# Merge stores of 64 rows, q and k laid channel by channel, and the merge weights on ScalarE's queue, in a dilated-attention decoder step

## The chip, the cores and the metric

The kernel is one program on one core of a Trainium2 chip. The metric is the device time of one execution in microseconds. The core has a matrix engine (TensorE, PE in the profile, with its weight loads as PEld), three engines for elementwise work (VectorE as DVE, ScalarE as ACT, GpSimd as POOL) and SyncE (SP), which here does nothing but issue transfers. Transfers run on sixteen DMA engines. SP and ACT can issue them; an issue stands in the issuing engine's instruction order, and an instruction that must wait holds up all that are behind it on its engine.

## What is computed

One layer of a decoder over a prompt of 2048 rows of 1024 and a sample group of 32 rows, all in fp32. The part that matters here is the attention of the prompt: eight heads of 64 channels, each with three dilated windows whose outputs are merged by their softmax denominators.

```python
q, k, v, u, vg = _project(x, norm1_g, w_in)
q, k, v = _heads(q), _heads(k), _heads(v)
for (w, d), bias_hj in zip(BRANCHES, biases):      # (128, 1), (512, 4), (2048, 16)
    o, l = _dilated_prompt(q, k, v, bias_hj, d, w // d + 1)
    outs.append(o)
    lses.append(l)
att = _merge_branches(outs, lses).reshape(B, S, D_ATT).astype(x.dtype)
...
x = x + jnp.concatenate([att, u * gate], axis=-1) @ w_out
x = x + _swiglu(x, norm2_g, w_gate, w_up, w_down)
```

## The kernel before

**Precision.** Operands of a matmul are split into a high part and a low remainder, and products of the parts are added up. q and k of a head are kept as parts of 64 channels each; a tile of 128 partitions holds two such parts, so that one matmul over 128 partitions gives two of the products. `qh` holds q's high part twice, `k` holds k's high and low part, `ql` holds q's low part twice. The sum over partitions does not depend on their order as long as all three tiles use the same one.

**Stages.** The input projection comes first (to about 661 us). It leaves q and k transposed in DRAM (`qk_d`, by part, 512 channels, 2048 positions), the values in `v_d`, and the gated half of the concatenation in `cat_d`. Then comes attention, head by head; then the output projection; then the feed-forward layer, which takes most of the rest.

**Attention.** A head is 20 items: 16 blocks of 128 queries of the first two windows together (the band; at most 640 keys each) and 4 strided items of the third window. Each item passes through scores (TensorE), bias and minimum (VectorE, lines 818 and 885 to 888, the last on GpSimd), exponential (ScalarE, lines 823 and 891), transposes (TensorE) whose results ScalarE and VectorE split into parts (`ph`, `pl`; lines 844 and 849), and products with the values (TensorE, lines 863 and 911). Four band blocks together give 512 columns of output. ScalarE copies them into `ob` (line 872): one tile of 128 x 2048 for each head, with two buffers, so head h writes the buffer that head h - 2 used. The upper and the lower 64 partitions of `ob` are products with the two parts of the values and are added much later, when the output projection reads them.

**The merge.** When a head's sums are complete, during the next head, two weights for each position are worked out (`weights_a`, `weights_b`), written to DRAM (`f_d`, line 959) and read back spread over all partitions, in four chunks of 512 positions (`merge_load`, line 967). GpSimd multiplies and adds for each chunk (lines 974 to 978), and `merge_store` (line 981) writes the chunk to `cat_d`.

**Order.** A planner holds (step, phase, function) and emits everything in that order, so the order on every engine is fixed when the program is built. One step is one item. Within a step the phases come as: early, exp, low, scores, turn, mid, values, out, misc, store. The loads of head h + 1 are emitted at steps 2 to 13 of head h, the merge of head h in steps 8 to 24 after its last item; that is, its last store stands at step 4 of head h + 2. All of these are transfers of SP's queue, one behind the other: loads of q, k, the bias table `b` and the values, the store of the weights, the merge loads and the merge stores.

**Output projection.** Eight units of 128 rows for each half of the columns of `w_out`. `load_cat` (line 1224) reads a block of `cat_d` in three transfers, `split_cat` adds the two halves and splits them. The first half of `w_out` is loaded during head 7 into `pair` buffers, the second half during the units, through the two `fr` buffers (line 1202). The last head is merged during these units, by VectorE and GpSimd in turn, chunk by chunk.

Of the kernel before, what the change touches and what calls it, by code (L numbers as in the profile page):

```python
# [10 lines left out]
F32 = mybir.dt.float32  # L11
# [8 lines left out]
P = 128  # L20
T = 2048
NT = T // P
D = 1024
KD = D // P
H = 8
C = 64
DA = 512
# [11 lines left out]
def dap(t, offset, pattern):  # L39
    return bass.AP(tensor=t.tensor, offset=t.offset + offset, ap=pattern)  # L40


class Plan:
# [21 lines left out]
def hymba_step(ctx: ExitStack, tc: tile.TileContext, A: dict, O: dict):  # L65
    nc = tc.nc
    sync, act, dve, pool, pe = nc.sync, nc.scalar, nc.vector, nc.gpsimd, nc.tensor
# [3 lines left out]
    dram = ctx.enter_context(tc.tile_pool(name="dram", bufs=1, space=DRAM))  # L71
# [27 lines left out]
    qk_d = dram.tile([2, 2, DA, T], F32, name="qk_d")  # L99
    v_d = dram.tile([T, H, 2, C], F32, name="v_d")  # L100

    cat_d = dram.tile([D + DA, T], F32, name="cat_d")
    f_d = dram.tile([H, 2, T], F32, name="f_d")
    l12_d = dram.tile([H, 768], F32, name="l12_d")
    l3_d = dram.tile([H, 256], F32, name="l3_d")
    b12_d = dram.tile([H, P, 640], F32, name="b12_d")
    b3_d = dram.tile([H, P, P], F32, name="b3_d")
    cs_d = dram.tile([SR, D], F32, name="cs_d")
    zs_d = dram.tile([3, SR, DA], F32, name="zs_d")

# [36 lines left out]
    at = plan.at  # L147
# [13 lines left out]
    def raw_tile():  # L161
        return rp.tile([P, 512], F32, name="raw", tag="raw", bufs=RAW)
# [141 lines left out]
    zn = {}  # L304
# [84 lines left out]
        act.activation(so, pt, AF.Copy)  # L389

    def store_gated(g, ct):
        sync.dma_start(cat_d[DA + ct * P:DA + (ct + 1) * P, g * 512:(g + 1) * 512], zn.pop(("so", g, ct)))

    def sample_rows(kind, ps):

# [53 lines left out]
        sync.dma_start(dst, l_)  # L449

    def table_spread():
        sync.dma_start(b12_d, dap(l12_d, 127, [[768, H], [-1, P], [1, 640]]))
        sync.dma_start(b3_d, dap(l3_d, 127, [[256, H], [-1, P], [1, P]]))
# [179 lines left out]
    for j in range(8):  # L633
        s0 = 105 + 4 * j if j < 3 else 117 + 3 * (j - 3) if j < 6 else 127 + 3 * (j - 6)
# [22 lines left out]
    for half in range(2):  # L657
        for ki, kind in enumerate(ORDER[half]):
            for gi, tiles in enumerate(GROUPS):
                start = ((half * 5 + ki) * 3 + gi) * 8  # L660
                for k in range(KD):
                    if start == 0:

                        for j in range(3):
                            n = 3 * k + j
# [6 lines left out]
                for j, tj in enumerate(tiles):  # L672
# [17 lines left out]
                    else:  # L690
# [24 lines left out]
    for i, (b, t, u) in enumerate(key_units):  # L715
        s0 = key_steps[i]
# [11 lines left out]
    for bg in range(2):  # L728
        s0 = V0 - 8 + bg * 33
# [31 lines left out]
    def value_tile(n):  # L761

        if n % 4 == 1:
            return hev.tile([P, NT, 2 * C], F32R, name="ve", tag="v", bufs=1)
        return hv.tile([P, NT, 2 * C], F32R, name="v", tag="v", bufs=3)

    def load_head(h):

        d = heads[h] = {}
        rows = slice(h * C, (h + 1) * C)  # L770
        qk = hev if h % 2 == 0 else hod
        for nm, w_, parts in (("qh", 0, (0, 0)), ("k", 1, (0, 1)), ("ql", 0, (1, 1))):
            t_ = d[nm] = qk.tile([P, T], F32R, name=nm, tag="qk", bufs=3)
            for s in range(2):
                sync.dma_start(t_[s * C:(s + 1) * C, :].bitcast(F32), qk_d[w_, parts[s], rows, :])
                yield
        b_ = row_tile("b")
        d["b3"], d["b12"] = b_[:, 640:768], b_[:, 0:640]
        sync.dma_start(d["b3"], b3_d[h])
        sync.dma_start(d["b12"], b12_d[h])  # L780
        yield
        if h == 0:

            t_ = d["vb"] = value_tile(2 * h + 1)
            for n0, n1 in ((0, 10), (10, NT)):
                sync.dma_start(t_[:, n0:n1].bitcast(F32), dap(v_d, n0 * P * H * 2 * C, [[H * 2 * C, P], [P * H * 2 * C, n1 - n0], [1, 2 * C]]))
                yield
# [168 lines left out]
        dve.tensor_mul(f[:, 0:2, :], f[:, 0:2, :], m.unsqueeze(1).broadcast_to([P, 2, NT]))  # L956

    def weights_store(h, f):
        sync.dma_start(dap(f_d, h * 2 * T, [[NT, P], [T, 2], [1, NT]]), f[:, 0:2, :])


    mf = {}

    def merge_load(h, ch):
        f1, f3 = mf[h, ch] = (raw_tile(), zn_tile())
        for z, t_ in enumerate((f1, f3)):
            sync.dma_start(t_, dap(f_d, (h * 2 + z) * T + ch * 512, [[0, P], [1, 512]]))

    def merge(h, ch, eng, part=None):
# [7 lines left out]
        if part in (None, 2):  # L977
            eng.tensor_add(x, x, y)

    def merge_store(h, ch):  # L980
        sync.dma_start(dap(cat_d, h * C * T + ch * 512, [[D * T, 2], [T, C], [1, 512]]), obs[h][:, ch * 512:(ch + 1) * 512])


    sgu = {}
# [48 lines left out]
    NI = len(OTHER)  # L1033
    L = B0 + len(items) - 1
    at(222, "misc", begin, 0)
    for y in range(7):
        at((222, 222, 224, 224, 226, 226, 228)[y], "misc", load, 0)
    at(232, "misc", load, 0)
    at(B0 + 3, "early", load, 0)
    at(B0 + 3, "store", load, 0)  # L1040
    for h in range(1, H):

        s0 = B0 + (h - 1) * NI
        at(s0 + 1, "misc", begin, h)
        for y in (2, 2, 3, 3, 4, 5, 5, 11, 13):
            at(s0 + y, "misc", load, h)
    for h in range(H):

        s0 = B0 + (h + 1) * NI
        end = h == H - 1  # L1050
        steps = ((2, "early"), (2, "turn"), (3, "early"), (4, "early"), (5, "early"), (5, "early")) if end else (
            (3, "misc"), (4, "misc"), (5, "early"), (6, "misc"), (7, "misc"), (7, "store"))
        for (y, ph), fn in zip(steps, (lambda h=h: stats_a(sts[h]), lambda h=h: stats_b(sts[h]), lambda h=h: stats_c(h, sts[h]),
                                       lambda h=h: fs.update({h: weights_a(h, sts[h])}), lambda h=h: weights_b(h, sts[h], fs[h]),
                                       lambda h=h: weights_store(h, fs[h]))):
            at(s0 + y, ph, fn)
        if not end:

            for ch, (a, b, c) in enumerate(((8, 11, 15), (8, 14, 18), (10, 17, 21), (14, 20, 24))):
                at(s0 + a, "misc", merge_load, h, ch)  # L1060
                for part in range(3):
# [137 lines left out]
    def load_wo(B, half, s2, staged):  # L1199
        raws["o", half, s2] = w_ = staged()  # L1200
        r0 = rows_of(2 * s2)
        sync.dma_start(w_.rearrange("p (a c) -> p a c", a=2),
                       A["w_out"][r0:r0 + 2 * P, half * 512:(half + 1) * 512].rearrange("(a p) c -> p a c", p=P))
# [188 lines left out]
    def last_load(ch):  # L1392

        x, m = last[ch] = (fraw(), None)
        for z, r0 in enumerate((3 * P, D + 3 * P)):
            sync.dma_start(x[:, z * 512:(z + 1) * 512], cat_d[r0:r0 + P, ch * 512:(ch + 1) * 512])

    def last_split(ch):
# [6 lines left out]
        else:  # L1405
            split_sb(B.xh[:, 7, 512:1024], B.xl[:, 7, 512:1024], x[:, 0:512], eng_lo=dve)

    at(L - 13, "early", last_head_free)
# [30 lines left out]
    at(U0 + 6, "misc", lambda: [sync.dma_start(g_, dap(A[nm], 0, [[0, P], [1, D]])) for g_, nm in zip(gain, ("norm2_g", "final_g"))])  # L1439
    for ch in range(2):  # L1440
        at(U0 + 7 + ch, "misc", last_load, ch)
# [202 lines left out]
```

## Time and profile before

| | |
|---|---|
| median of 3 runs | 2908.54 us (2903.59 to 2911.81) |
| profiled execution | 2907.21 us |
| its span | 2905.4 us |
| mean granted TensorE clock | 0.958 |
| PE / PEld busy | 92% / 78% |
| DVE / ACT / POOL busy | 41% / 26% / 29% |
| DMA queue of SP | 356.38 MB, 39.9% of sixteen engines' span |
| DMA queue of ACT | 8.92 MB, 1.2% |

The span runs from the first to the last instruction. A busy share is a mean over stages with different limits. A line number is that of the kernel before; where a helper does the work for several callers it is the helper's line. A wait is told as what waited, for what, the sum, how often, and the longest.

### The profile page before, as it was taken

What the parts mean: (1) busy time and instruction counts of PE and PEld (TensorE: products, weight loads), DVE (VectorE), ACT (ScalarE), POOL (GpSimd) and SP (SyncE); (2) the same over time, 40 slices, a digit from 0 to 9 for tenths busy, and PEclk for the clock granted to TensorE, in tenths of its full rate; (3) what the DMA queues carried; (4) which work ended last, traced back from release to release, by engine and by line L of the source; (5) the groups of instructions that cost most, each with busy time, mean ns of one, the idle gap of its engine ahead of it and who ended that gap; (6) DMA issues with size and microseconds to landing.
All of it is one profiled execution on the core that took longest, in us unless ns stands there. A gap on an engine that the chain in (4) does not pass through costs nothing.

```text
span 2905.4 us, 33754 instructions
## 1 busy us (share of the span) xinstructions
PE 2680.6 (92%) x13058; PEld 2256.7 (78%) x13058; DVE 1198.6 (41%) x2287; ACT 762.7 (26%) x1426; POOL 848.9 (29%) x558
## 2 busy tenths in 40 slices
PE   8988888988887885999999999997999999999997
PEld 6776666667886773788888888875799999999996
DVE  3267774325766663522222222244432222222224
ACT  5323243435665661301000100022310000000002
POOL 1034642121432442122332232211032222222222
PEclk9999999998998887999999999998999999999999
DMA  7754834577665645232232223226132222222211
GB/s 239 214 177 137 265 108 132 179 207 200 170 171 151 181 144 163 95 102 87 100 104 100 87 94 110 87 76 206 39 116 88 94 95 88 87 87 87 88 44 60
DMA packets 290565, 367.45 MB, mean 126 GB/s; under 512 B 19399, under 2 KB 216184, under 8 KB 285284
## 3 DMA queue, kind: packets, MB, share of 16 engines
q1 hardware_dynamic: 285284, 356.38, 39.9%
q10 hardware_dynamic: 5120, 8.92, 1.2%
q8 instruction: 103, 1.69, 0.2%
q14 instruction: 58, 0.48, 0.1%
HBM read 309.88 MB, written 125.47 MB: 150 GB/s over the span
## 4 chain that ended last, share of the span: by engine, by line
PE 68%; DVE 10%; DMA 7%; ACT 4%; issue 3%; SPq 2%; POOL 1%; ACTq 0%; DVEq 0%; POOLq 0%
PE ps_o L1336 17%; PE ps_s L1310 12%; PE ps_s L1311 11%; PE ps_s L1312 11%; DVE pl L849 2%; PE ps_o L863 2%; PE ps_s L296 1%; DMA fr<-in_w_out_dram 1%; PE ps_s L297 1%; PE ps_s L298 1%; DVE e L818 1%; PE ps_s L812 1%; PE ps_o L1250 1%; PE ps_o L1252 1%; PE ps_o L1251 1%
## 5 line engine op out<-in xcount | busy, mean ns | idle before, releaser
L1310 PE MATMUL ps_s<-xh,gh 128*128 128x352 f32 (+1 forms) x1760 | 624.1, 355 | 0.0
L1312 PE MATMUL ps_s<-xh,gl 128*128 128x352 f32 (+1 forms) x1760 | 620.3, 352 | 0.0
L1311 PE MATMUL ps_s<-xl,gh 128*128 128x352 f32 (+1 forms) x1760 | 619.5, 352 | 0.0
L1336 PE MATMUL ps_o<-dw,hw 128*128 128x512 f32 x2112 | 500.9, 397 | 8.6 <-DVE acc L1338 8.5
L1336 PEld LDWEIGHTS ps_o<-dw,hw 128*128 128x128 f32 x2112 | 396.5, 189 | 108.1 <-DVE acc L1338 14.5
L1314 ACT ACTIVATE zn<-ps_s 128x352 f32<-128x352 f32 (+1 forms) x110 | 57.1, 519 | 1319.0 <-PE ps_s L1312 1319.0
L1315 DVE TENSOR_TENSOR zn<-zn,ps_s 128x352 f32<-128x352 f32 (+1 forms) x110 | 64.6, 588 | 722.4 <-ACT zn L1314 722.4
L1310 PEld LDWEIGHTS ps_s<-xh,gh 128*128 128x128 f32 x1760 | 332.0, 189 | 33.5
L1311 PEld LDWEIGHTS ps_s<-xl,gh 128*128 128x128 f32 x1760 | 331.2, 188 | 31.6
L1312 PEld LDWEIGHTS ps_s<-xh,gl 128*128 128x128 f32 x1760 | 330.3, 188 | 32.4
L1338 DVE TENSOR_TENSOR acc<-acc,ps_o 128x512 f32<-128x512 f32 x352 | 241.0, 687 | 214.6 <-PE ps_o L1336 214.6
L126 POOL TENSOR_TENSOR hw<-zn,hw 128x512 fp32r<-128x512 f32 (+2 forms) x110 | 119.8, 1089 | 662.0 <-DVE hw L125 662.0
L126 POOL TENSOR_TENSOR gl<-fr,gh 128x1024 fp32r<-128x1024 f32 x88 | 212.8, 2442 | 131.4 <-ACT gh L123 131.4
L126 POOL TENSOR_TENSOR dw<-fr,dw 128x1024 fp32r<-128x1024 f32 x44 | 106.5, 2420 | 377.7 <-DVE dw L125 377.7
L296 PE MATMUL ps_s<-wh,xh 128*128 128x512 f32 x480 | 200.6, 418 | 7.6 <-ACT xh L123 6.4
L297 PE MATMUL ps_s<-wl,xh 128*128 128x512 f32 x480 | 194.8, 406 | 5.6 <-DVE wl L208 5.6
L298 PE MATMUL ps_s<-wh,xl 128*128 128x512 f32 x480 | 193.8, 404 | 0.0
L296 PEld LDWEIGHTS ps_s<-wh,xh 128*128 128x128 f32 x480 | 94.5, 197 | 38.1 <-issue 9.2
L297 PEld LDWEIGHTS ps_s<-wl,xh 128*128 128x128 f32 x480 | 94.8, 198 | 25.0 <-DVE wl L208 7.4
L298 PEld LDWEIGHTS ps_s<-wh,xl 128*128 128x128 f32 x480 | 94.3, 196 | 21.3 <-DVE xl L126 0.2
L849 DVE TENSOR_TENSOR pl<-ps_t,ph 128x384 fp32r<-128x384 f32 (+2 forms) x152 | 69.5, 475 | 77.8 <-ACT ph L844 77.7
L823 ACT ACTIVATE e<-e,st 128x640 f32<-128x640 f32 (+4 forms) x128 | 96.3, 752 | 2.1 <-DVE st L818 2.0
(323 smaller groups left out, 4084.3 us busy)
## 6 DMA issues: line engine op xcount, KB each, us to landing
out_ks_dram<-in_cache_k_dram SPq DMA_DIRECT2D x56, 512.0 KB
out_vs_dram<-in_cache_v_dram SPq DMA_DIRECT2D x56, 512.0 KB
fr<-in_w_gate_dram SPq DMA_DIRECT2D x44, 512.0 KB
fr<-in_w_up_dram SPq DMA_DIRECT2D x44, 512.0 KB
fr<-in_w_down_dram SPq DMA_DIRECT2D x44, 512.0 KB
raw<-in_w_in_dram SPq DMA_DIRECT2D x72, 256.0 KB
qk_d<-pair SPq DMA_DIRECT2D x64, 256.0 KB
kv<-in_cache_k_dram SPq DMA_DIRECT2D x64, 192.0 KB
```

The lines of the kernel that those rows point to most:

```text
L126: (eng_lo or pool).tensor_sub(lo, src, hi.bitcast(F32))
L296: pe.matmul(o[j], xh[:, k, :], wh, start=(k == 0), stop=False)
L297: pe.matmul(o[j], xh[:, k, :], wl, start=False, stop=False)
L298: pe.matmul(o[j], xl[:, k, :], wh, start=False, stop=(k == KD - 1))
L823: act.activation(e[:, 0:w], e[:, 0:w], AF.Exp, bias=st[:, 0, n:n + 1], scale=-1.0, accum_out=st[:, 1, n:n + 1])
L849: dve.tensor_sub(lo, p, hi.bitcast(F32))
L1310: pe.matmul(ps[:, q_, 0:n], wh[:, ks], B.xh[:, k, a:b], start=(k == 0), stop=False)
L1311: pe.matmul(ps[:, q_, 0:n], wh[:, ks], B.xl[:, k, a:b], start=False, stop=False)
L1312: pe.matmul(ps[:, q_, 0:n], wl[:, ks], B.xh[:, k, a:b], start=False, stop=(k == KD - 1))
L1315: dve.tensor_mul(sg[:, 0:n], sg[:, 0:n], ps[:, 1, 0:n])
L1336: pe.matmul(ps[0:nr], l_, r_[:, cs], start=(z == 0 and y == 0), stop=(z == FC - 1 and y == len(ops) - 1))
L1338: dve.tensor_add(B.acc[i][0:nr, cs], B.acc[i][0:nr, cs], ps[0:nr])
```

## The change

- `merge_store` writes a whole head at once (the last head still by chunks), in two transfers: 64 rows of the upper and 64 of the lower half of `ob`. Before, each chunk was one transfer whose outermost dimension was the two halves.
- `load_head` loads each of `qh`, `k` and `ql` in one transfer to 128 partitions. The two parts of a channel lie in neighbouring partitions; before, each part was a transfer to 64 partitions. The bias tables of a head lie together in DRAM (`b_d`) and are one transfer.
- `weights_store` and, for heads 0 to 6, `merge_load` are issued by ACT. A merge load brings both weights of a chunk in one transfer, into a `pair` buffer (two of them).
- Steps: loads of q, k, b at 1 to 4 and of the values at 13 and 15; the weights one to two steps earlier; merge loads at 11, 11, 16 and 19, the merge parts from 13, 16, 19 and 22 (two later), the store at 25.
- The rows of `cat_d` are reordered (gated part first), so `load_cat` reads gated and merged rows in one transfer and the low part in a second.
- The first half of `w_out` passes through a value buffer in place of `pair`, with its loads and splits at other steps.

A head then has 13 transfers in place of 23: 3 for q and k, 1 for b, 2 for values, 1 to store and 4 to load weights, 2 to store the merged output.

```diff
-    b12_d = dram.tile([H, P, 640], F32, name="b12_d")
-    b3_d = dram.tile([H, P, P], F32, name="b3_d")
+    b_d = dram.tile([H, P, 768], F32, name="b_d")
...
-            for s in range(2):
-                sync.dma_start(t_[s * C:(s + 1) * C, :].bitcast(F32), qk_d[w_, parts[s], rows, :])
-                yield
+            sync.dma_start(t_.bitcast(F32), dap(qk_d, ((w_ * 2 + parts[0]) * DA + h * C) * T,
+                                                [[T, C], [(parts[1] - parts[0]) * DA * T, 2], [1, T]]))
+            yield
...
-        sync.dma_start(d["b3"], b3_d[h])
-        sync.dma_start(d["b12"], b12_d[h])
+        sync.dma_start(b_[:, 0:768], b_d[h])
...
     def weights_store(h, f):
-        sync.dma_start(dap(f_d, h * 2 * T, [[NT, P], [T, 2], [1, NT]]), f[:, 0:2, :])
+        act.dma_start(dap(f_d, h * 2 * T, [[NT, P], [T, 2], [1, NT]]), f[:, 0:2, :])
...
     def merge_load(h, ch):
-        f1, f3 = mf[h, ch] = (raw_tile(), zn_tile())
-        for z, t_ in enumerate((f1, f3)):
+        if h < H - 1:
+            f = pair_tile(F32)
+            mf[h, ch] = (f[:, 0], f[:, 1])
+            act.dma_start(f, dap(f_d, h * 2 * T + ch * 512, [[0, P], [T, 2], [1, 512]]))
+            return
+        mf[h, ch] = (raw_tile(), zn_tile())
+        for z, t_ in enumerate(mf[h, ch]):
             sync.dma_start(t_, dap(f_d, (h * 2 + z) * T + ch * 512, [[0, P], [1, 512]]))
...
-    def merge_store(h, ch):
-        sync.dma_start(dap(cat_d, h * C * T + ch * 512, [[D * T, 2], [T, C], [1, 512]]), obs[h][:, ch * 512:(ch + 1) * 512])
+    def merge_store(h, c0, c1):
+        for z in range(2):
+            r0 = DA * (z + 1) + h * C
+            sync.dma_start(cat_d[r0:r0 + C, c0 * 512:c1 * 512], obs[h][z * C:(z + 1) * C, c0 * 512:c1 * 512])
...
-        for y in (2, 2, 3, 3, 4, 5, 5, 11, 13):
+        for y in (1, 2, 3, 4, 13, 15):
             at(s0 + y, "misc", load, h)
...
-            (3, "misc"), (4, "misc"), (5, "early"), (6, "misc"), (7, "misc"), (7, "store"))
+            (2, "misc"), (3, "misc"), (4, "early"), (4, "misc"), (5, "misc"), (6, "mid"))
...
-            for ch, (a, b, c) in enumerate(((8, 11, 15), (8, 14, 18), (10, 17, 21), (14, 20, 24))):
-                at(s0 + a, "misc", merge_load, h, ch)
+            for ch, (a, b) in enumerate(((11, 13), (11, 16), (16, 19), (19, 22))):
+                at(s0 + a, "mid", merge_load, h, ch)
                 for part in range(3):
                     at(s0 + b + part, "store", merge, h, ch, pool, part)
-                at(s0 + c, "store", merge_store, h, ch)
+            at(s0 + 25, "store", merge_store, h, 0, 4)
...
-        for dst, r0, n in ((parts[0], DA, 4), (parts[1], 0, na), (m, D, na)):
+        for dst, r0, n in ((parts[0], 0, 4), (parts[1], DA, na), (m, D, na)) if staged else ((r, 0, ns), (m, D, na)):
             sync.dma_start(dst[:, 0:n], cat_d[r0:r0 + n * P, t0:t0 + P].rearrange("(s p) t -> p s t", p=P))
...
+    def first_stage(s2):
+        if s2 == 0:
+            stage["w"] = value_tile(2 * H).rearrange("p n c -> p (n c)").bitcast(F32)
+        return stage["w"][:, s2 % 2 * D:(s2 % 2 + 1) * D]
...
-    for s2 in range(4):
-        at(L - 12 + 3 * s2, "misc", load_wo, B, 0, s2, square_tile)
-        at(L - 9 + 3 * s2, "misc", split_wo, B, 0, s2, gate_tiles)
+    for s2, (a, b) in enumerate(((-12, -9), (-12, -7), (-8, -4), (-6, -2))):
+        at(L + a, "misc", lambda s2=s2: load_wo(B, 0, s2, lambda: first_stage(s2)))
+        at(L + b, "misc", split_wo, B, 0, s2, gate_tiles)
...
-        at(U0 + s + 1, "misc", merge_store, h, ch)
+        at(U0 + s + 1, "misc", merge_store, h, ch, ch + 1)
```

More of the change, by code (lines that the diff above doesn't have):

```diff
@@ L391, in store_gated @@
     def store_gated(g, ct):
-        sync.dma_start(cat_d[DA + ct * P:DA + (ct + 1) * P, g * 512:(g + 1) * 512], zn.pop(("so", g, ct)))
+        sync.dma_start(cat_d[ct * P:(ct + 1) * P, g * 512:(g + 1) * 512], zn.pop(("so", g, ct)))
     def sample_rows(kind, ps):
@@ L451, in table_spread @@
     def table_spread():
-        sync.dma_start(b12_d, dap(l12_d, 127, [[768, H], [-1, P], [1, 640]]))
-        sync.dma_start(b3_d, dap(l3_d, 127, [[256, H], [-1, P], [1, P]]))
+        sync.dma_start(b_d[:, :, 0:640], dap(l12_d, 127, [[768, H], [-1, P], [1, 640]]))
+        sync.dma_start(b_d[:, :, 640:768], dap(l3_d, 127, [[256, H], [-1, P], [1, P]]))
     def sample_table_load():
@@ L769, in load_head @@
         d = heads[h] = {}
-        rows = slice(h * C, (h + 1) * C)
         qk = hev if h % 2 == 0 else hod
@@ L1035, in hymba_step @@
     at(222, "misc", begin, 0)
-    for y in range(7):
-        at((222, 222, 224, 224, 226, 226, 228)[y], "misc", load, 0)
+    for y in (222, 224, 226, 228):
+        at(y, "misc", load, 0)
     at(232, "misc", load, 0)
@@ L1394, in last_load @@
         x, m = last[ch] = (fraw(), None)
-        for z, r0 in enumerate((3 * P, D + 3 * P)):
+        for z, r0 in enumerate((DA + 3 * P, D + 3 * P)):
             sync.dma_start(x[:, z * 512:(z + 1) * 512], cat_d[r0:r0 + P, ch * 512:(ch + 1) * 512])
@@ L1406, in last_split @@
             split_sb(B.xh[:, 7, 512:1024], B.xl[:, 7, 512:1024], x[:, 0:512], eng_lo=dve)
+    stage = {}
+    def first_stage(s2):
+        if s2 == 0:
+            stage["w"] = value_tile(2 * H).rearrange("p n c -> p (n c)").bitcast(F32)
+        return stage["w"][:, s2 % 2 * D:(s2 % 2 + 1) * D]
     at(L - 13, "early", last_head_free)
-    for s2 in range(4):
-        at(L - 12 + 3 * s2, "misc", load_wo, B, 0, s2, square_tile)
-        at(L - 9 + 3 * s2, "misc", split_wo, B, 0, s2, gate_tiles)
+    for s2, (a, b) in enumerate(((-12, -9), (-12, -7), (-8, -4), (-6, -2))):
+        at(L + a, "misc", lambda s2=s2: load_wo(B, 0, s2, lambda: first_stage(s2)))
+        at(L + b, "misc", split_wo, B, 0, s2, gate_tiles)
     at(L + 1, "misc", lambda: load_cat(B, 0, 7, (raw_tile(), raw_tile(), zn_tile())))
```

## The prediction

> **What bounds the kernel now.** I read the busy time by stretches first, then who waited for whom in the attention stage, then the transfer queue's own timeline, then the chain of waits around the out-projection. The changed functions work only in two of these stretches: attention (661 to about 1075 us) and the out-projection behind it (to about 1200 us); the feed-forward stage from there on is untouched. By stretches (window; its length, then busy time of PE, weight load, DVE, ACT, POOL; then the granted clock, the busy share of the 16 DMA engines, and GB/s):
>
> ```profile
> span 2905.4 us, 33754 instructions
> ...
> 940.00:990.00 50.00, 42.47 (x266) 38.67 (x265) 34.13 (x87) 31.72 (x77) 19.28 (x16) 0.91 0.68 175
> 1120.00:1160.00 40.00, 11.23 (x39) 8.05 (x39) 7.06 (x7) 3.89 (x4) 9.99 (x5) 0.68 0.42 146
> 735.00:738.00 3.00, 3.00 (x24) 3.00 (x23) 1.88 (x5) 2.64 (x7) 2.26 (x2) 1.00 1.03 340
> 766.00:771.00 5.00, 5.00 (x37) 4.95 (x36) 4.28 (x13) 4.43 (x11) 0.00 (x0) 1.00 0.98 210
> 782.50:792.70 10.20, 9.36 (x37) 8.82 (x38) 5.96 (x13) 6.56 (x15) 3.36 (x3) 0.50 0.58 166
> 1012.00:1022.00 10.00, 9.45 (x64) 8.50 (x62) 7.46 (x20) 7.48 (x19) 7.35 (x6) 1.00 0.14 54
> ```
>
> TensorE sets the pace in both, and it has holes: 7.5 us in 940 to 990, 28.8 us in 1120 to 1160. The last four rows are what transfers cost. In 735 to 738 rows of 2 KB go to 128 partitions at 340 GB/s with all engines busy. In 766 to 771 only q and k parts are moving, 64 partitions a transfer, and the same full engines give 210 GB/s. In 1012 to 1022 mostly merge stores are left, and a share of 0.14 is two engines of sixteen. And behind a hole the clock is at 0.50 for 10 us. The holes in attention have one cause:
>
> ```profile
> PEld ps_o L911 <- ACT ob L872: 32.2, 6, 7.7
> PE ps_o L911 <- ACT ob L872: 30.9, 6, 7.5
> ```
>
> PE waits (31 us of idle time, seen by both its halves; us in total, times, longest) for ScalarE's copy of the first band outputs into ob. That copy has a long wait of its own. On the transfer queue, then ScalarE, for head 6:
>
> ```profile
> 955.61 7.76 SPq L981 DMA_DIRECT2D cat_d<-ob  x3
> 963.46 3.71 SPq L775 DMA_DIRECT2D qh<-qk_d  x2
> 967.26 1.18 SPq L775 DMA_DIRECT2D k<-qk_d  x2
> 968.50 0.59 SPq L775 DMA_DIRECT2D ql<-qk_d  x1
> 969.18 0.53 SPq L981 DMA_DIRECT2D cat_d<-ob  x1
> 969.82 9.31 SPq L775 DMA_DIRECT2D ql<-qk_d  x1
> ```
> ```profile
> 969.18 22.15 DMA cat_d<-ob
> ...
> 991.44 0.60 ACT L872 ACTIVATE ob<-ps_o 128x512 f32<-128x512 f32 x1 [9.17 <-DMA cat_d<-ob]
> ```
>
> ob has two buffers, so head 6 may write its ob only when head 4's last store has landed. That store of 256 KB takes 22 us: it stands behind three others on the same two engines (a store alone at 54 GB/s is 4.9 us) and behind five half-loads of q and k. ScalarE stands from 982.27 to 991.44.
>
> What a head costs without this is read from DVE, whose bias instruction over 128 columns opens each head:
>
> ```profile
> 757.17 0.28 DVE L818 CUSTOM_DVE_ANT_0 e<-ps_s,b 128x128 f32<-128x128 f32 x1
> ...
> 962.62 0.28 DVE L818 CUSTOM_DVE_ANT_0 e<-ps_s,b 128x128 f32<-128x128 f32 x1
> ...
> 1014.71 0.81 DVE L818 CUSTOM_DVE_ANT_0 e<-ps_s,b 128x640 f32<-128x640 f32 x1
> ...
> 1016.05 0.28 DVE L818 CUSTOM_DVE_ANT_0 e<-ps_s,b 128x128 f32<-128x128 f32 x1
> ...
> 1059.15 0.81 DVE L818 CUSTOM_DVE_ANT_0 e<-ps_s,b 128x640 f32<-128x640 f32 x1
> ```
>
> ```profile
> L818 DVE CUSTOM_DVE_ANT_0 e<-ps_s,b x128: 278/812/817, 662.1 to 1059.2; 128x640 f32<-128x640 f32 x96, 128x128 f32<-128x128 f32 x8, 128x256 f32<-128x256 f32 x8, 128x384 f32<-128x384 f32 x8
> ```
>
> Head 7, which loads no further head and so does not wait, takes 43.1 us from first to last of them; 1.3 us more (1014.71 to 1016.05) leads to the next head: 44.4. Heads 2 to 6 take 258.9 together, 51.8 each. The surplus is 258.9 - 5 x 44.4 = 36.9 us: the wait itself and the slow clock behind it.
>
> **The change part by part.** *Merge store.* Four stores of 128 rows of 2 KB (outer dimension 2) become two of 64 rows of 8 KB, one step later, when all four chunks are merged. The nearest row for 64 partitions and 8 KB is 766 to 771: 210 GB/s with all engines at work, so 1.05 MB takes 5.0 us and not four times 4.9. Bounds: 340 GB/s (3.1 us) if the halves overlap, 54 GB/s (19.4 us) if the engines are again two; I take 210, the row of the same shape. The Trainium skill (DMA: Bandwidth & Descriptors, "Why a DMA increments its semaphore by 16 and not by 1") gives the engine count as the largest number up to 16 that divides the slowest dimension of both sides: 2 before, 16 after. By it the store goes as here, by the two-engine row as in rival 4; the share of 0.14 agrees with its 2.
>
> *q and k.* Six transfers to 64 partitions become three to 128, channels of both parts alternating; 3.15 MB at 210 is 15.0 us, at 340 it is 9.3. No row shows 8 KB rows to 128 partitions; 340 has the same partitions, 210 the same row length. I take 340: a longer row is no reason for a slower transfer, so the halved partitions are the likelier cause of the 210. The Trainium skill (SBUF — State Buffer, "Door 1: The DMA port swizzle") has 64 partitions reach only 8 of the 16 ports, which would make the 128-partition transfer about twice as fast; 210 against 340 leans that way.
>
> ```profile
> 1140.89 0.38 SPq L1202 DMA_DIRECT2D fr<-in_w_out_dram  x1
> ```
> ```profile
> 1144.40 1.06 ACT L123 ACTIVATE woh<-fr 128x1024 fp32r<-128x1024 f32 x1 [6.89 <-DMA fr<-in_w_out_dram]
> ```
>
> *When does the store land?* Times from the head's first bias. SP can issue q and k when the head before has made its last scores, about -2 (its last bias instruction stands at -1.3, 1014.71 above); at 340 they and the 0.39 MB of bias are through by -2 + 10.5 = +9. Beside its bytes a transfer takes some 2 us: w_out in the next stage is issued at 1140.89 and awaited to 1144.40, and 0.52 MB at 340 are 1.5 of these 3.5. The last merge now needs POOL's work two steps later, behind the strided subtraction:
>
> ```profile
> 965.41 1.29 POOL L978 TENSOR_TENSOR ob<-ob,o 128x512 f32<-128x512 f32 x1
> 969.65 1.06 POOL L888 TENSOR_TENSOR e<-e,st 128x512 f32<-128x512 f32 x1 [2.95 <-DVE st L887]
> ```
>
> That subtraction ends at 970.71, +8.1; two merge parts of 1.3 follow, so the store is issued at +11, moves until +16.5, and lands at +18.5 with the 2 us of completion. ScalarE asks at 982.27, +19.7, and PE notices only 2 us after that (the wait is 9.17 long, PE's longest 7.5). So the wait goes, with 1 to 3 us to spare. At 210 for q and k they end at +15, the store at +22: ScalarE would stand 2.5 us, PE hardly 1. Gain here: 36.9 us. The lower bound is a loss: with two engines the store lands at +32.5 where it now lands at 991.33, +28.7, and 3.8 us over five heads are 19. The upper bound has heads 0 and 1 also at 44.4 (they take 757.2 - 662.1 = 95.1 together, 6 over): 43.
>
> *Weights store and merge loads on ScalarE.* Five issues a head, in an in-order engine with the exponentials and the ph copies behind them, on which PE's values wait.
>
> ```profile
> L497 ACTq DMA_DIRECT2D qb<-zs_d x32: 357/358/602, 142.1 to 375.0; - x32
> L123 ACT ACTIVATE gh<-pair x4: 1043/1058/1079, 1035.6 to 1059.5; 128x1024 fp32r<-128x1024 f32 x4
> ```
>
> At 0.36 us an issue it is 1.8 us a head, 12.6 for seven heads if nothing hides it. ScalarE is idle 18 us of the 50 above, half of it the wait itself, and head 7, my yardstick, carries four copies of 1.06 us that other heads don't have: I take 0 beyond the yardstick, and 12.6 as the end of the range. SP loses 15 issues a head; it bounds nothing but the loads it holds back, which is counted above.
>
> *Order of loads.* Values come two steps later and are used in the next head; b is one transfer; statistics move one or two steps ahead at their old distances. The first half of w_out is staged in a value buffer because pair now holds the merge weights; its splits end two steps earlier. The bias tables of DRAM move the same bytes in the same rows. All 0; without cover the largest is a value load (1.05 MB, 3.1 us, once a head).
>
> *Out-projection.* Here the last head still stores by chunk, and the same two engines hold up what is queued behind:
>
> ```profile
> 1116.23 1.04 SPq L981 DMA_DIRECT2D cat_d<-ob  x2
> 1117.31 5.51 SPq L967 DMA_DIRECT2D raw<-f_d  x1
> ...
> 1124.70 0.38 SPq L1202 DMA_DIRECT2D fr<-in_w_out_dram  x1
> ...
> 1141.37 1.04 SPq L981 DMA_DIRECT2D cat_d<-ob  x2
> 1142.46 4.43 SPq L1439 DMA_DIRECT2D norm_g<-in_norm_g_dram  x1
> ...
> 1147.56 0.51 SPq L1202 DMA_DIRECT2D fr<-in_w_out_dram  x1
> ```
> ```profile
> 1135.20 1.06 ACT L123 ACTIVATE wol<-fr 128x1024 fp32r<-128x1024 f32 x1 [22.62 <-DMA fr<-in_w_out_dram]
> ...
> 1159.18 1.06 ACT L123 ACTIVATE wol<-fr 128x1024 fp32r<-128x1024 f32 x1 [13.71 <-DMA fr<-in_w_out_dram]
> ```
>
> With two more store issues (1 us) but no 5.51, w_out is issued at about 1120. The data ahead of it since 1114 and itself, 3.3 MB (one cat load, one x block, stores, merge weights), is 10.6 us: it lands at 1126 and not 1135, -9. The next follows POOL's subtraction behind it, also 9 earlier; then four store issues and two gains take 3.5 us instead of 6.7, and 2.6 MB, 7.7 us, land by 1140 and not 1159: -19 in all. PE then finds its clock down as before. I take -18; ends -8 (only the two long issues go) and -24 (the 28.8 idle us above, less one load's 5). The unstaged cat loads lose one issue of 0.5 us each, 15 of them; I take -1.
>
> Sum against the profiled 2907.2 (span 2905.4 and 1.8 around it; 1.3 below the median of the runs shown): 2907 - 37 - 18 - 1 = **2851 us**.
>
> **The rivals.**
> 1. *The stall shrinks only.* The store moves a step later and in one piece, so if POOL or the loads are late it lands near +25, ScalarE stands 5 us and PE 3, and the clock still drops. Of 36.9 about 20 stay: 2871. For it: a margin of 1 to 3 us. Against: two bounds for the loads both end before +22.
> 2. *ScalarE inherits the waits.* Its merge load waits for the landed weights store, and the third and fourth for POOL to give back a pair buffer.
>
> ```profile
> SPq L967 <- DMA f_d<-f: 57.0, 7, 12.0
> POOL ob L974 <- DMA raw<-f_d: 81.7, 6, 16.9
> ```
>
> SP waited up to 12 us for that landing and POOL up to 16.9 us for merge weights; on SP this harmed little, on ScalarE it stops the softmax. The store is now issued near +10 and asked for near +20, so 12 us would cost 2 us; with some POOL lateness 4 us a head: 7 x 4 = 28 given back, 2879. By the Trainium skill (DMA: Bandwidth & Descriptors, "Issuing engines are not separate DMA queues") all queues share the sixteen engines, which speaks for this one; that the engines are idle by then speaks against.
> 3. *Slower.* The same place at its worst: if merge weights issued at +20 take 20 us to land, POOL frees the first pair buffer two parts later, at +42.6, and ScalarE, which asks for it at step 16, near +32, stands 10 us a head: +70 against -56, 2921. It decides from 8 us a head (56 / 7). For it: the 16.9 above. Against: 0.5 MB at 340 GB/s is 1.6 us.
> 4. *It doesn't do what it says.* If 64 rows still go by two engines, the 1.05 MB takes 19.4 us, all at the end: the 19 us of loss above and no gain in the out-projection, 2926. Against: the 64-row loads kept all engines busy.
>
> **How the numbers follow.** Forecast 0.65 (2851), rival 1 0.15, rival 2 0.14, rival 3 0.04, rival 4 0.02. The likeliest's own range: 2834 (43 and 24 gained, and 6 for a clock that stays up) to 2866 (the 12.6 unhidden, or the smaller gain in the out-projection). Reaching into rivals 1 and 2 gives 2834 to 2882. Faster than 0.3% (9 us, what can be told here from no change): 0.91; within 0.03, the far end of rival 2; slower 0.06, rivals 3 and 4.
>
> **What would show it.** Two cat_d<-ob transfers a head; no ScalarE wait on them at L872's counterpart; heads 1 to 6 at 43 to 46 us from first bias to first bias; q and k stretches near 340 GB/s; no half clock in the middle of heads; PE busy well over 11 us in the forty that now hold 28.8 idle. Wrong, if ScalarE shows multi-microsecond waits before a merge load, if stores keep a share near 0.14, or if the heads stay over 48.

## The result

The changed kernel takes 2872.4 us (median of 4 runs, 2870.4 to 2874.0) against 2906.1 us for the one before on the same chip (4 runs, 2903.6 to 2911.8): a ratio of 0.9881, 95% interval 0.9863 to 0.9899. It is faster, by 33.7 us; the forecast was 2851. The profiled execution took 2874.0 us with a span of 2872.2, which is 33.2 below the span of before.

Where the time went is read as before, by stretches (window; length; busy time of PE, weight load, DVE, ACT, POOL; granted clock; share of the 16 DMA engines; GB/s). Kernel after:

```profile
span 2872.2 us, 33608 instructions
...
940.00:990.00 50.00, 44.76 (x287) 41.39 (x286) 35.11 (x91) 34.98 (x84) 21.29 (x19) 0.93 0.60 177
953.00:960.00 7.00, 6.91 (x40) 6.12 (x40) 6.04 (x19) 3.45 (x11) 0.99 (x1) 1.00 0.96 356
964.00:971.00 7.00, 6.25 (x29) 6.26 (x30) 3.33 (x7) 5.48 (x13) 2.54 (x3) 0.55 0.50 109
1120.00:1160.00 40.00, 37.49 (x158) 29.30 (x157) 19.17 (x36) 12.04 (x21) 4.74 (x2) 0.94 0.38 122
```

The out-projection window that held 11.23 us of PE work now holds 37.49 (all of that stage has also moved forward). q, k and the bias move at 356 GB/s, not 210. But the attention window has gained only 2.3 us of PE work, and there is still a stretch at a clock of 0.55. The waits of the attention stage (650 to 1075 us) say what became of the old stall and what is new (waiting instruction, what it waited for; us in total, times, longest). Kernel after:

```profile
POOL ob L977 <- DMA pair<-f_d: 24.0, 3, 8.7
...
ACT e L889 <- POOL e L886: 21.9, 6, 4.5
...
PE ps_t L898 <- ACT e L889: 10.4, 4, 3.3
...
POOL ob L977 <- DVE f L953: 7.0, 1, 7.0
...
POOL ob L977 <- DVE dd L950: 6.3, 1, 6.3
...
ACT ob L870 <- PE ps_o L861: 5.4, 11, 1.5
```

The copy into ob (L870, L872 before) no longer waits for any store, so the old stall is gone. In its place POOL waits for merge weights, ScalarE's strided exponential (L889) for POOL, and PE's transposes (L898) for ScalarE. The waits of 7.0 and 6.3 us, in heads 4 and 5, stand at the same merge as the other three. The profile puts them down to DVE, but that merge reads only the loaded weights and `ob`, so they count with the 24.0: 37.3 us in five waits. In head 6, in order of time, first SP's and ScalarE's queue, then the engines:

```profile
947.79 0.56 SPq L773 DMA_DIRECT2D qh<-qk_d  x1
948.44 0.56 SPq L773 DMA_DIRECT2D k<-qk_d  x1
949.05 0.60 SPq L773 DMA_DIRECT2D ql<-qk_d  x1
...
966.64 1.12 SPq L986 DMA_DIRECT2D cat_d<-ob  x2
```
```profile
948.74 0.37 ACTq L966 DMA_DIRECT2D pair<-f_d  x1
```
```profile
961.77 1.26 POOL L977 TENSOR_TENSOR ob<-ob,pair 128x512 f32<-128x512 f32 x1 [7.78 <-DMA pair<-f_d]
962.99 1.04 POOL L886 TENSOR_TENSOR e<-e,st 128x512 f32<-128x512 f32 x1
```
```profile
964.06 0.63 ACT L889 ACTIVATE e<-e 128x512 f32<-128x512 f32 x1 [4.52 <-POOL e L886]
```
```profile
964.75 1.11 PE L898 MATMUL ps_t<-ident,e 128*128 128x128 f32 x4 [3.31 <-ACT e L889]
```

This is the new wait from end to end. The merge weights of the last chunk (0.5 MB) are issued at 948.74, among 3.15 MB of q and k of the next head, and POOL can use them 13.0 us later, at 961.77. POOL executes in order; behind this merge stands the subtraction L886, which the softmax of the running head needs. So ScalarE stands 4.5 us, PE 3.3, and then the clock falls (964 to 971 above). It happens once in each of heads 2 to 6.

A head is timed as in the prediction, from DVE's bias instructions; the out-projection by DVE's twenty-fourth sum (L1258 before, L1263 after). Kernel after, then before:

```profile
760.59 0.28 DVE L816 CUSTOM_DVE_ANT_0 e<-ps_s,b 128x128 f32<-128x128 f32 x1
...
999.11 0.28 DVE L816 CUSTOM_DVE_ANT_0 e<-ps_s,b 128x128 f32<-128x128 f32 x1
...
1043.97 0.81 DVE L816 CUSTOM_DVE_ANT_0 e<-ps_s,b 128x640 f32<-128x640 f32 x1
...
1185.47 0.68 DVE L1263 TENSOR_TENSOR acc<-acc,ps_o 128x512 f32<-128x512 f32 x1
```
```profile
1217.94 0.68 DVE L1258 TENSOR_TENSOR acc<-acc,ps_o 128x512 f32<-128x512 f32 x1
```

Heads 2 to 6 take 999.11 - 760.59 = 238.5 us (258.9 before), head 7 takes 44.9 (43.1), and from head 7's last bias to the sum are 1185.47 - 1043.97 = 141.5 (1217.94 - 1059.15 = 158.8). The same three stretches were read in the profile of every experiment; the names of the kernels are explained in the next section, each where it is described:

| kernel | median us | ratio to before (95%) | heads 2 to 6 | head 7 | out-projection |
|---|---|---|---|---|---|
| before | 2906.1 | | 258.9 | 43.1 | 158.8 |
| after | 2872.4 | 0.9881 (0.9863 to 0.9899) | 238.5 | 44.9 | 141.5 |
| store_only | 2854.1 | 0.9812 (0.9795 to 0.9829) | 218.1 | 43.1 | 139.4 |
| qk_only | 2879.7 | 0.9901 (0.9885 to 0.9918) | 235.2 | 43.1 | 158.7 |
| store_and_qk | 2848.0 | 0.9789 (0.9771 to 0.9807) | 218.1 | 43.1 | 142.2 |
| two_engines_heads | 2969.5 | 1.0211 (1.0190 to 1.0232) | 306.6 | 59.9 | 159.3 |
| two_engines_last | 2881.5 | 0.9913 (0.9892 to 0.9935) | 238.1 | 45.5 | 156.0 |
| merge_earlier | 2853.1 | 0.9809 (0.9794 to 0.9825) | 218.4 | 46.3 | 140.3 |
| merge_behind | 2862.7 | 0.9847 (0.9833 to 0.9862) | 228.5 | 46.6 | 141.5 |
| qk_later | 2853.9 | 0.9819 (0.9804 to 0.9833) | 222.9 | 45.5 | 140.1 |
| merge_on_sp | 2856.9 | 0.9827 (0.9813 to 0.9842) | 220.4 | 45.9 | 146.3 |
| store_and_split_order | 2848.2 | 0.9791 (0.9776 to 0.9805) | 218.2 | 43.1 | 141.2 |
| earlier_and_split_order | 2850.3 | 0.9799 (0.9783 to 0.9815) | 218.3 | 46.2 | 135.9 |
| store_order_merge | 2850.6 | 0.9794 (0.9781 to 0.9808) | 218.3 | 43.1 | 138.0 |

### The profile page after: what moved, and what is told of

Read it like the earlier page. It is cut to its first block, busy times and chain, and to the rows that moved or that the text cites. A ratio compares the mean times of both kernels' runs of the same rounds, so it can differ in the third digit from the quotient of the medians.

```text
span 2872.2 us, 33608 instructions
## 1 busy us (share of the span) xinstructions
PE 2680.6 (93%) x13058; PEld 2260.2 (79%) x13058; DVE 1197.0 (42%) x2287; ACT 762.5 (27%) x1426; POOL 849.5 (30%) x558
## 4 chain that ended last, share of the span: by engine, by line
PE 71%; DVE 8%; DMA 6%; ACT 4%; issue 4%; POOL 2%; SPq 1%; ACTq 0%; POOLq 0%; DVEq 0%
PE ps_o L1341 17%; PE ps_s L1315 12%; PE ps_s L1316 12%; PE ps_s L1317 12%; PE ps_s L295 2%; PE ps_s L296 2%; PE ps_s L297 2%; DVE pl L847 1%; PE ps_o L1255 1%; PE ps_o L1257 1%; PE ps_o L1256 1%; PE ps_s L810 1%; DMA fr<-in_w_out_dram 1%; PE ps_o L861 1%; PE ps_t L838 1%
## 5 line engine op out<-in xcount | busy, mean ns | idle before, releaser
L816 DVE CUSTOM_DVE_ANT_0 e<-ps_s,b 128x640 f32<-128x640 f32 (+4 forms) x128 | 93.4, 730 | 3.8 <-PE ps_s L810 3.8
```

The source lines that it names most:

```text
L816: dve.tensor_tensor_reduce(e[:, 0:w], s[:, c0:c0 + w], d["b12"][:, 640 - w:640], 1.0, BIG, OP.add, OP.min, st[:, 0, n:n + 1])
```

## The experiments

**The store alone** (store_only). The kernel before with one edit:

```
 def merge_store(h, ch):
-    sync.dma_start(dap(cat_d, h * C * T + ch * 512, [[D * T, 2], [T, C], [1, 512]]), obs[h][:, ch * 512:(ch + 1) * 512])
+    for z in range(2):
+        r0 = D * z + h * C
+        sync.dma_start(cat_d[r0:r0 + C, ch * 512:(ch + 1) * 512], obs[h][z * C:(z + 1) * C, ch * 512:(ch + 1) * 512])
```

> The kernel before, with one edit: each chunk's merge store goes as two transfers of 64 rows (2 KB a row), and nothing else of the change. Theory S (the store on two engines is the cause of both old losses): no ScalarE wait for cat_d<-ob of more than 1 us, PE's 30.9 us of wait for it gone, the DMA share in 1012 to 1022 far from 0.14, the half clock behind those waits gone; 35 us from attention and 15 from the out-projection, 2852 to 2862 us, which is faster than the whole change. Rival Q (the q and k loads ahead of the store count as much): they still run at about 210 GB/s, the store lands late by 3 to 6 us, about half the wait stays, 2875 to 2885 us.

Measured: 2854.1 us, 18 us faster than the whole change. ScalarE's waits in attention, a stretch where q and k move, and the window 940 to 990 of this kernel:

```profile
ACT ob L872 <- PE ps_o L863: 7.8, 20, 1.1
```
```profile
940.00:990.00 50.00, 47.81 (x301) 43.01 (x301) 38.12 (x99) 35.73 (x87) 21.12 (x18) 0.97 0.76 193
...
944.00:952.00 8.00, 7.95 (x58) 7.63 (x56) 6.50 (x24) 6.56 (x16) 0.71 (x1) 1.00 0.99 208
```

The stall is gone although q and k still crawl at 208 GB/s: PE's busy time goes from 42.47 to 47.81 us of 50, and a head takes 218.1 / 5 = 43.6 us. Theory S holds.

**q and k alone** (qk_only). The kernel before with the three 128-partition loads of the change.

> The kernel before, with only the q and k loads laid channel by channel over 128 partitions. Theory S (the two-engine stores are the cause): the loads take 9.3 us a head instead of 15, the last store lands some 5 us sooner, PE's wait of 5 to 7 us a head shrinks to 0 to 3 and the out-projection stays as before: 2880 to 2892 us. Rival Q (the loads alone held the store): the wait in attention goes altogether, 2868 to 2875 us. Rival N (stores on two engines are the floor whatever is loaded): 2900 us or more.

```profile
PE ps_o L912 <- ACT ob L873: 7.5, 5, 2.3
```

Measured: 2879.7 us, at the edge of what theory S gave. PE's wait in heads 2 to 6 falls from 30.2 us (the 30.9 less 0.7 at the end of head 7) to 7.5, and the out-projection gains nothing (158.7). The faster loads only shorten the queue ahead of a store that remains slow.

**Both of them** (store_and_qk), without the rest of the change.

> The kernel before with two edits of the change: the merge store as two transfers of 64 rows a chunk, and q and k over 128 partitions; loads, merges and queues stay as before. Theory S (once the store has sixteen engines the loads' lay-out no longer lies on the path): the same as with the store alone, 2850 to 2857 us, heads 2 to 6 at 43 to 44. Rival Q (the two gains add, 28 us of the loads alone on top of 54): below 2845 us.

Measured: 2848.0 us, between what theory S and rival Q gave. Heads 2 to 6 take 218.1 us with or without the new q and k loads, so on top of the store these are worth nothing there. The medians differ by 6 us, but the intervals overlap: whether it is faster than the store alone was not settled. What it does show is the price of the remaining parts: the whole change is 24 us slower than these two of its parts.

**The store back on two engines**, in the kernel after, first in heads 0 to 6 (two_engines_heads), then in head 7 (two_engines_last):

```
 def merge_store(h, c0, c1):
+    if h < H - 1:        # second kernel: h == H - 1
+        sync.dma_start(dap(cat_d, (DA + h * C) * T + c0 * 512, [[DA * T, 2], [T, C], [1, (c1 - c0) * 512]]), obs[h][:, c0 * 512:c1 * 512])
+        return
```

> The kernel after, but heads 0 to 6 store their merged output as one transfer of outer dimension 2 (1.05 MB, rows of 8 KB). Theory S: the transfer takes about 19.4 us at 54 GB/s, lands near +35 after the head's first bias, ScalarE stands about 15 us at the first band output of heads 2 to 6, heads 53 us or more: 2872 plus 5 x 8 to 5 x 13, 2910 to 2940 us. Rival Q (the new q and k loads alone took the wait away): 2880 us at most, heads within 1.5 us of the kernel after.

> The kernel after, but head 7 stores its four chunks as one transfer each of outer dimension 2; heads 0 to 6 as in the kernel after. It prices the out-projection term by itself. Theory S: the two-engine backlog returns there, the second w_out split comes back to about 32 us behind where it now is less what attention gave, so 2872 + 16 = 2888 us (2880 to 2892), attention unchanged. Rival: the out-projection gained by the other edits (w_out staged in a value buffer, fewer issues), then 2872 within 4 us.

The first took 2969.5 us, 97 more than the kernel after and 30 above the worst that was expected. Its store in head 6, the copy into ob that needs it, and the end of that stretch:

```profile
1013.34 0.55 SPq L985 DMA_DIRECT2D cat_d<-ob  x1
```
```profile
1036.07 0.60 ACT L870 ACTIVATE ob<-ps_o 128x512 f32<-128x512 f32 x1 [12.65 <-DMA cat_d<-ob]
```
```profile
1022.00:1030.00 8.00, 2.67 (x21) 2.32 (x19) 2.82 (x7) 1.42 (x4) 0.00 (x0) 1.00 0.13 53
```

A share of 0.13 and 53 GB/s are again two engines; the store is waited for until 22.7 us after its issue. It was issued 15.5 us after the head's first bias (997.81), because POOL is late here too, so the two delays add, and ScalarE stands 12.65 us. Even the out-projection is back at 159.3: head 6's store is issued only at 1130.05 us, after the last bias of head 7 (1119.97), so its backlog reaches into that stage.

The second took 2881.5 us, 9.1 more by the medians. By stage the out-projection goes from 141.5 to 156.0, so 14.5 of the 17.3 us gained there hang on the store of the last head. The profiled runs differ by only 5.5 us, because the stages ahead of attention, the same code in both, took 9.4 us less in this one (first bias at 653.8 us, in the kernel after at 663.2). Whether the medians too differ by less than 14.5 for that reason is not shown.

**The merges two steps earlier** (merge_earlier), which issues the last merge load ahead of q and k:

```
-for ch, (a, b) in enumerate(((11, 13), (11, 16), (16, 19), (19, 22))):
+for ch, (a, b) in enumerate(((9, 11), (9, 14), (14, 17), (17, 20))):
...
-at(s0 + 25, "store", merge_store, h, 0, 4)
+at(s0 + 23, "store", merge_store, h, 0, 4)
```

> The kernel after, with all four merge loads, merges and the store of heads 0 to 6 two steps earlier, so that the last merge load is issued some 4.8 us sooner, ahead of the next head's q and k loads. Theory G (what attention did not gain is POOL, standing in order at the last chunk's merge for a load that shares the engines with q and k, with the strided subtraction behind it): POOL's wait of 7.8 us in heads 2 to 6 is gone, PE's gaps of 1.9 to 3.3 us and the half clock behind them too, heads at 44 to 45.5, 2872 - 17 = 2855 us (2850 to 2860). Rival A (the five issues on ScalarE hold the heads at 47.7): no change, 2870 to 2874. Rival F: the first merge load now comes too close to the weights store, the wait moves to chunk 0, 2865 to 2880.

Waits in attention, and POOL at the first chunk of a head:

```profile
POOL ob L977 <- DMA pair<-f_d: 34.1, 9, 6.1
...
ACT e L889 <- POOL e L886: 2.1, 2, 1.2
```
```profile
951.92 1.04 POOL L886 TENSOR_TENSOR e<-e,st 128x512 f32<-128x512 f32 x1 [8.68 <-DVE st L885]
957.88 1.30 POOL L977 TENSOR_TENSOR ob<-ob,pair 128x512 f32<-128x512 f32 x1 [4.92 <-DMA pair<-f_d]
```

Measured: 2853.1 us, 19 less than the kernel after; heads 2 to 6 take 218.4. Rival F was right about the first chunk: POOL now waits there for most of its 34.1 us. But the subtraction stands ahead of that merge, so ScalarE's wait falls from 21.9 to 2.1 us. It is not the length of POOL's wait that costs, but what stands behind it.

**Only the order on POOL** (merge_behind): the last chunk's three parts behind the subtraction, its load where it was.

```
-... (16, 19), (19, 22))):            +... (16, 19), (19, 23))):
-at(s0 + 25, "store", ...)            +at(s0 + 26, "store", ...)
```

> The kernel after, with only the three POOL parts of the last chunk's merge one step later (and the store one step later), so that in POOL's order they stand behind the strided subtraction; the merge load itself stays where it is. Theory G (the late load costs time only because POOL, in order, stands before the subtraction that the softmax needs): POOL still waits about 8 us for the load, but behind the subtraction, ACT's and PE's gaps at the strided exponential and transposes are gone, 2853 to 2858 us. Rival L (the late load itself, or the later store, is what costs): ScalarE now waits for the store at the first band output, 2865 us or more.

```profile
945.34 1.04 POOL L886 TENSOR_TENSOR e<-e,st 128x512 f32<-128x512 f32 x1 [5.52 <-DVE s L936]
949.14 1.29 POOL L977 TENSOR_TENSOR ob<-ob,pair 128x512 f32<-128x512 f32 x1 [2.77 <-DMA pair<-f_d]
```

Measured: 2862.7 us, between what the two theories gave. The load, issued at 935.85, still serves only at 949.14, 13.3 us later, but the subtraction no longer waits behind it; half of the 20 us comes back. Of the other half the trace shows a part: the late store, for which ScalarE stands again at the first copy into ob. The profile puts 3.1 us in two waits down to it. Two more, of 1.5 and 2.2 us, stand at the same copy in other heads and end 6.8 and 6.7 us after the store's issue, as one of the first two does (6.7), so 6.8 us in four waits are likelier. The rest of it stays open.

**Only the company of the load** (qk_later): q, k and bias loads five steps later, behind the store.

```
-for y in (1, 2, 3, 4, 13, 15):
+for y in (6, 7, 8, 9, 13, 15):
```

> The kernel after, with the next head's q, k and bias loads five steps later, behind the merge store on SP's queue (they are used 20 steps later). Theory G with contention: the last merge load, now alone on the engines, lands some 4 us after its issue instead of 13, POOL's wait and PE's gaps go, the store too finds free engines: 2853 to 2858 us. Rival T (a 128-fold broadcast read is slow whatever moves beside it): the load still takes over 10 us and the time stays at 2870 to 2874. Rival V (the loads now collide with the weights store, the next merge loads and the values): 2860 to 2885.

```profile
941.61 1.28 POOL L977 TENSOR_TENSOR ob<-ob,pair 128x512 f32<-128x512 f32 x1 [1.03 <-DMA pair<-f_d]
```

Measured: 2853.9 us. Without q and k beside it the last merge load serves 5.0 us after its issue at 936.59, instead of 13.0. So it is the sharing that made it slow, and not its 128-fold broadcast (rival T). The Trainium skill (DMA: Bandwidth & Descriptors, "Issuing engines are not separate DMA queues") says that transfers of all issuing engines run on the same sixteen engines and interleave; 13.0 against 5.0 us on ScalarE's own queue agrees. Heads 2 to 6 take 222.9, so some 4 of the 20 us stay; what they are was not followed up.

**The loads back on SP's queue** (merge_on_sp), at the same steps (the two calls of act.dma_start become sync.dma_start for the weights store and the merge loads).

> The kernel after, with the weights store and the merge loads of heads 0 to 6 issued by SP instead of ScalarE, at the same steps. Theory G: SP's order puts the last merge load ahead of the next head's q and k loads, so it no longer shares the engines with them; POOL's wait goes, 2853 to 2860 us, and ScalarE's 1.8 us of issues a head make no further difference. Rival A (the issues on ScalarE are what cost): the same gain but with heads under the 44.4 us of the earlier yardstick, 2850 or less. Rival W (SP now stands at each merge load for the weights store or a free buffer and holds the q, k and value loads behind it): 2875 to 2900.

Measured: 2856.9 us; heads 2 to 6 take 220.4, and no POOL wait for the merge weights is left among the larger waits of heads 2 to 6. On one queue the last merge load is issued ahead of q and k. With ScalarE issuing, and early enough, the heads take 218.4: its 1.8 us of issues a head cost nothing that can be seen. Rival A falls by the time, which it had at 2850 or less, though the heads, 44.1 us each, are under 44.4 as it said.

**What is left in the out-projection.** With the store alone PE still stands 9.87 us in one piece. Three orders were tried: later splits of w_out on the store alone (store_and_split_order) and on the earlier merges (earlier_and_split_order), and on the first of these also a later merge of head 7 (store_order_merge).

```
-for s2, s, e in ((0, 3, 4), (1, 4, 5), (2, 5, 6), (3, 6, 7)):
+for s2, s, e in ((0, 3, 4), (1, 4, 6), (2, 5, 7), (3, 6, 7)):
...
-for ch, s, eng in ((0, 3, dve), (1, 3, pool), (2, 5, dve), (3, 5, pool)):      # third kernel only
+for ch, s, eng in ((0, 3, dve), (1, 3, pool), (2, 6, dve), (3, 6, pool)):
```

> The kernel before with the two-transfer store, and in the out-projection the splits of the second and third part of w_out's second half one step later, so that ScalarE makes the last unit's own input first and does not stand before it for w_out. Theory O (what is left in the out-projection is ScalarE, in order, standing for w_out ahead of the split that PE needs: PE idle 9.9 us in one piece): most of that gap goes, 1 to 3 us return as a wait at the second half's first unit, 2846 us (2843 to 2850). Rival P (the wait only moves, PE waits as long for w_out at the second half): 2852 to 2856.

> The kernel after with the merges of heads 0 to 6 two steps earlier and the same later splits of w_out. Theory O: 2853 less 6 to 9 us, 2846 us (2843 to 2849). Rival P: 2851 to 2855. It also tells whether the change's other parts are worth anything once neither store nor merge waits: then this one is more than 3 us below the kernel with the store alone and the same splits.

> The kernel before with the two-transfer store, the later splits of w_out, and head 7's merge of its third and fourth chunk one step later, behind the last unit's own input on DVE. Theory M (the gap of 9.3 us that the later splits left is DVE, in order, standing 8.7 us for merge weights ahead of the sum of that input): the gap goes to under 2 us, some of it returns at the second half's first unit, which waits for w_out; the time from head 7's last bias to the twenty-fourth output sum falls from 141 to 134 to 137 us, 2842 to 2846 us. Rival P (the input itself comes late, or the wait moves again as a whole): 2847 to 2852.

Measured: 2848.2, 2850.3 and 2850.6 us. PE's gap with the store alone, then with the later splits, then the waits of 1075 to 1115 us with both edits:

```profile
1093.34 0.79 PE L1252 MATMUL ps_o<-gh,xh 128*128 128x512 f32 x1 [9.87 <-ACT xh L123]
```
```profile
1091.82 0.80 PE L1252 MATMUL ps_o<-gh,xh 128*128 128x512 f32 x1 [9.30 <-ACT xh L123]
```
```profile
PE ps_o L1253 <- POOL wol L126: 8.6, 2, 7.0
```

Each edit moves the wait to the next in line: from ScalarE, standing for w_out, to DVE, standing for the merge weights, to POOL's low part of w_out at the second half. The first time lies in theory O's range, but a gap that stays at 9.30 is what rival P had; the third is as rival P had it, though its gap did go. Nor is earlier_and_split_order, with the other parts of the change, faster than store_and_split_order: its out-projection is 5.3 us shorter, but its head 7 is 3.1 longer. The seven kernels from 2848 to 2854 us can't be told apart by their intervals. All of them beat both given kernels: two parts of the change without the rest give 0.9789 of the time before.

## Why the prediction was right or wrong

**The number.** 2872.4 lies 21 us above the forecast and outside the forecast's own range, 2834 to 2866. It lies within 2834 to 2882 only because that range reaches into rivals 1 and 2, and neither of their mechanisms occurred: that much of the agreement is luck. Of the signs that were named, those for the store, for q and k and for the out-projection came. Heads at 43 to 46 us without a half clock did not: heads 1 to 6 took 46.4 to 50.8, heads 1 to 3 of them over the 48 that was to show the prediction wrong, and the clock was still at 0.55 from 964 to 971.

**The stall and its cause: right.** Heads 2 to 6 were to lose their surplus of 36.9 us over 44.4 each. With the store alone they lose 258.9 - 218.1 = 40.8. The Trainium skill (DMA: Bandwidth & Descriptors, "Why a DMA increments its semaphore by 16 and not by 1") gave two engines for the old store; the 0.13 and 53 GB/s of the store put back agree.

**q and k at 340: right** (356 measured), but not needed on the path. The old lay-out cost 24 us of waiting only because the store was slow (qk_only), and nothing in the heads once it was fast.

**When the store lands: the issue was mis-sized, the outcome right.** It went out at 966.64 - 951.28 = 15.4 us after the head's first bias and not at +11, since POOL was late; the ob copy still did not wait.

**The step that failed** is in the same part: "The last merge now needs POOL's work two steps later, behind the strided subtraction." It took POOL's place in the order and never asked when the merge weights would be there. The part on ScalarE counted what its issues cost ScalarE, and gave the SP queue's lost order no price: on SP the last merge load went ahead of the next head's q and k, on ScalarE it runs among them. Rival 3 looked at this load and dismissed it with 0.5 MB at 340 GB/s, 1.6 us; in company it took 13.0. The missing term is what merge_earlier gives back, 238.5 - 218.4 = 20.1 us; against the 44.4 a head of the forecast it is 238.5 - 222 = 16.5. What is late next when the stall goes was asked for the store, and not for the subtraction queued behind the merge.

**Rival 2 named the right transfer and the wrong engine.** Nowhere did ScalarE stand for microseconds at a merge load; POOL, in order, carried the wait to it. Rival 1's 2871 lies next to the measured 2872, but its mechanism, ScalarE standing for a late store, did not occur. Rival 4's price, 2926, was too low: with two engines in heads 0 to 6 alone it is 2969.5. The store also goes out later than +11 (at +15.5 in head 6), and head 7 stands for one too (59.9 us, before 43.1).

**ScalarE's issues at 0 beyond the yardstick: right** (0.37 us each in the trace; 218.4 with them, 220.4 without). **Out-projection -18 and cat loads -1**: -17.3 together, of which 14.5 are shown to come from the store. The sum: 16.5 from the failed step, 4.0 from head 1 (50.8 us, before 48.6) and head 7, 1.7 in the out-projection and 0.5 in the stages outside are 22.7 of the 22.8 us between forecast and the profiled time. Head 1 needs no cause in the change: in store_only and store_order_merge, which are the same up to there, it takes 48.6 and 51.0. Head 7 takes 44.9 to 46.6 us in the kernels that have the whole change (59.9 with two engines in the heads before it) and 43.1 in all others; the new staging of w_out, whose splits fall into it, may be why, but that was not tried.

**Slips in the working** that change nothing here: 3.3 MB at 340 GB/s are 9.7 us and not 10.6; the two terms named for the range's upper end give 2864 and 2861, and not 2866; and in 735 to 738 not only rows of 2 KB move, for value loads in pieces of 512 bytes were issued at 733.80 and 734.49.

## What to carry to other kernels

When a transfer is moved to another engine's queue, ask what the old queue kept ahead of it: an order that nobody wrote down (merge weights ahead of q and k) was worth 20 us here. When an in-order engine must wait for a load, put behind everything urgent the instruction that waits, or issue the load before the big transfers; POOL waits 34 us for merge weights in merge_earlier, and 37 us in the kernel after: in the first it costs nothing, in the second 20 us. And measure the parts of a change alone: one edit of four lines, the shape of a store, gave more than the whole.

## What the hardware showed that was not expected

The same 0.5 MB read took 13.0 us on ScalarE's queue while 3.15 MB moved on SP's, and at most 5.0 without them. At the 356 GB/s seen there, q, k, the bias and this read together (4.1 MB) are 11.4 us, an estimate: so the small read is ready about as late as if it stood behind all the others, when the DMA engines fall idle (a share of 0.02 in 961 to 964). Why it is not served sooner stays open. A store of 1.05 MB on two engines was awaited until 22.7 us after its issue, where its bytes at 54 GB/s are 19.4; what the other 3 us are was not separated. And the stages ahead of attention, the same code in all kernels that were made from the one after, ended between 653.8 and 663.2 us in their profiled runs, which is why the stages above are compared each by itself.
